# Readout scratch, two-part triangles, modulation on ScalarE and the order of fills in a two-layer diffusion block

## The chip, the cores and the metric

One Trainium2 chip; the program runs on one of its cores. The metric is device time of one execution in microseconds (us). The median of three executions of the kernel before is 2352.65 us.

## The reference

Two layers of a diffusion block over 512 latent tokens and 256 context tokens (together 768 columns), width 1024, all in fp32:

```python
def trunk_layer(x, xc, c, c_ctx, ada_w, ada_b, norm_g, w_in, ..., ctx_out):
    mod = jax.nn.silu(c) @ ada_w + ada_b
    mod_c = jax.nn.silu(c_ctx) @ ada_w + ada_b
    shift, scale, gate = jnp.split(mod[:, None, :], 3, axis=-1)
    ...
    h = rms_norm(x, norm_g) * (1.0 + scale) + shift
    za, ga, zb, gb, zc, gc, zg = jnp.split(h @ w_in, list(IN_CUTS), axis=-1)
    ya, yac = rwkv7_branch(za, zac, ...)            # recurrence, both directions
    yb = dense_block_attention(qb_, k of zbc and zb, v of zbc and zb)       # MLA
    yc = window_attention(qc_, kc_, vc_, kcc, vcc, c_sink)                  # GQA
    x_new = x + gate * merge_branches((ya, yb, yc), (ga, gb, gc), zg, w_branch_out, w_out)
    ...                                             # the same for the context, in layer 0 only

def rwkv7_scan(r, decay, k, v, kk, a, s0, reverse):
    def step(S, inp):
        r_t, w_t, k_t, v_t, kk_t, a_t = inp
        sa = jnp.einsum('bhvk,bhk->bhv', S, kk_t)
        S = (S * w_t[:, :, None, :] - sa[..., None] * (kk_t * a_t)[:, :, None, :]
             + v_t[..., None] * k_t[:, :, None, :])
        return S, jnp.einsum('bhvk,bhk->bhv', S, r_t)
    ...
```

Each branch output is multiplied by its own SiLU gate (`ga`, `gb`, `gc`), projected, weighted by sigmoid gates of `zg`, summed and projected once more.

## The kernel before

**Stages of a layer.** `head` makes the modulated input `hh`, `hl` (a high and a low part; every large product is made of three, high by high, high by low, low by high). `zphase` makes the inputs of the recurrence. `rwkv` runs the recurrence in 12 chunks of 64 steps, both directions and all heads at once. Then come MLA (`mla`), GQA (`gqa`), the projections of the branches and the last projection (`tail`).

**Fills.** The projections that nobody needs at once are a list of tiles (`todo` in `tiles`, lines 1457 to 1467): `zb` (MLA), `zc` (GQA), the gate tiles `ga`, `gb`, `gc` and 24 tiles of `zg`. A tile is 8 pieces; in the second layer a piece is 3 products of 128x512 for most tiles. `pace(n)` (line 1471) traces the next n pieces at the point where it is called, to give TensorE work while the other engines prepare something. `FILL` (line 33) says how many at which point: 72 and 56 in the second layer before the chunk loop begins, then per chunk at three stops. A raw tile is read from PSUM by ScalarE (line 778); a SiLU tile by ScalarE and then VectorE (lines 780, 782).

**Order.** A scheduler orders the instructions of each engine when the program is compiled: among those that it holds to be ready, the one with the lowest band number goes first (`band(SERVE)` before `band(B + 1)`, and so on to `B + 4` for fills); emission order decides only inside a band. The engines then work their queues in order. Two things bind the order further. `tc.issue_after(x)` ties what is traced inside behind x on x's engine. And `in_line()` (line 148) ties every product on TensorE behind the product traced just before it, whatever stage that belonged to, since `line["last"]` is set by every product and every transposition of the program:

```python
    def queued(i):
        if line["on"] and line["last"] is not None:
            tc.add_manual_dep(i.ins, line["last"].name, ...)
        line["last"] = i.ins
```

The chunk loop of `rwkv` and the last steps of the first inverse run inside `in_line()` (line 538).

**The recurrence.** For each chunk, `rwkv_scores` loads `BK`, `AR` and `UV` (lines 611 to 625) on SP's queue and makes the scores (`scps`); `rwkv_step` makes `Rp`, `Up`, `Sp` and `Yp`. Scores run two chunks ahead of the step. `AR` has 4 places, and so has `UV`. `rwkv_inverse` inverts the triangles of four chunks: it loads them as `TT` (lines 659 to 664, four loads), transposes the two diagonal 32x32 blocks on VectorE (670), eliminates in 30 steps of two VectorE instructions (676 to 681), transposes (684, 685), and then TensorE makes the block below the diagonal (`zp`, line 694, reading the other block of `TT`, and `yp`, line 702). One `TT` place, so the next group's load waits for the last `zp`. The first inverse runs in band B + 1 before the loop, the others in band B + 2.

`readout` (line 567) normalises finished columns, after chunks 3, 9 and 11 in the first layer and 9 and 11 in the second. Its scratch `tmp` (line 578) takes one `AR` place; its loads of `bvd` and the gate take `UV` places (599).

**Modulation.** `ada` (line 224) makes the modulation. With `pool` (before the first `head`) it works in 512 columns; otherwise, as `side`, in 16 halves of 256 columns that are stepped along between the pieces of other products in the first layer: 8 products `modps`, a VectorE copy to `row` (261), 4 transpositions `modpt`, and a VectorE addition of the bias into `mod` (269 or 272). `modps` and `modpt` share one PSUM place.

**GQA tokens.** `gqa_tokens` (line 1115, second layer called at line 1493 in band B + 3, before `rwkv`) takes six blocks of 128 tokens; in the second layer blocks 0 and 1 have keys and values only. Per block: loads `raw` from `zb_d` (1161, two places) on SP, transpositions `gqm` (1169), squares on ScalarE into `x` (1172), sums and rotation on VectorE (1173, 1143, 1147) and POOL (1149), a store of `x` (1177). In the second layer `x`, its helper and the PSUM place are single.

Of the kernel before, what the change touches and what calls it, by code (L numbers as in the profile page):

```python
# [10 lines left out]
F32 = mybir.dt.float32  # L11
# [3 lines left out]
ALU = mybir.AluOpType  # L15
# [4 lines left out]
P = 128  # L20
# [11 lines left out]

FILL = ((48, 48, 2, (2, 2, 2), (3, 3, 3), 2), (72, 56, 4, (2, 2, 2), (3, 3, 3), 2))

# [26 lines left out]
def build(tc, A, out):  # L61
# [162 lines left out]
    def ada(l, pp, mod, parts, pool=None):  # L224
# [25 lines left out]
        for q, h in [(q, h) for q in parts for h in range(512 // n)]:  # L250
            ps = bank([P, n], "modps")

            for k0 in range(0, KT, 4):
                with band(SERVE):
                    ws = four(q, h, k0)
                    for i in range(4):
                        mm(ps[32 * i:32 * i + 32], sc2[:, k0 + i, :], ws[i], start=(k0 == 0), stop=(k0 + 4 == KT),
                           skip_group_check=True)
                yield
            row = spool.tile([P, T], F32, tag="st", name="row", bufs=2)  # L260
            V.tensor_copy(row[:, 0:n], ps)
            nf = n // P
            pt = bank([P, nf, 2], "modpt")
            for i in range(nf):
                mm(pt[:, i, :], row[:, i * P:(i + 1) * P], C["sum4"])
            if q < 4:
                m, b = (a.rearrange("p (s f) c -> p s f c", s=2)[:, h:h + nf // 2, 2 * q:2 * q + 2]
                        for a in (mod[:, 0:16], pp[:, o:o + 16].unsqueeze(2)))
                V.tensor_tensor(m, pt.rearrange("p (s f) c -> p s f c", s=nf // 2), b.to_broadcast([P, nf // 2, 2, 2]), ALU.add)
            else:  # L270
                f = 4 * q + 2 * h
                V.tensor_tensor(mod[:, f:f + nf], pt, pp[:, o + f:o + f + nf].unsqueeze(2).to_broadcast([P, nf, 2]), ALU.add)

# [235 lines left out]

    def rwkv(l, D, last, DL, B, pace, zlast):  # L510

        with tc.tile_pool(name="rw", bufs=1, reuse_waits="tile") as rp:
# [23 lines left out]
            with band(B + 4), tc.issue_after(zlast):  # L536
                pace(FILL[l][1])
            with band(B + 1), in_line():
                for _ in ahead:
                    pace(FILL[l][2])  # L540
                ahead = out = iter(())
                for i in range(NCH):
# [9 lines left out]
                    step = rwkv_step(l, last, i, yo, st, DL, rp, parts.pop(i), YB[i // NS])  # L552
                    for n in FILL[l][3 if i % NS < NS - 1 else 4]:
                        next(step, None)
                        next(nxt, None)
                        if i % NS == NS - 1:
                            next(ahead, None)
                        next(out, None)
                        pace(n)
# [7 lines left out]
    def readout(l, D, rp, yo, part):  # L567
# [9 lines left out]

        tmp = rp.tile([P, 6, 256], F32, tag="AR", name="ro", bufs=4)
        def spread(p):
            ps = psum_bcast(256)  # L580
            mm(ps, bones, tmp[:, 4 + p % 2])
            V.tensor_scalar(tmp[:, p], ps, 1.0 / 64, None, ALU.mult)

        for p in range(4):
            y = cols(yo[:, p])
            ps = psum_bcast(256)
            mm(ps, C["center"], y)
            S.copy(y, like(ps, y))
            S.activation(like(tmp[:, 4 + p % 2], y), y, AF.Square)
            if p:  # L590
                spread(p - 1)
            yield
# [64 lines left out]
    def rwkv_inverse(l, rp, g, YB):  # L657

        TT = rp.tile([P, 8, NS, 64], F32, tag="TT", name="TT")
        cs = slice(g * NS, (g + 1) * NS)  # L660
        for b0 in (0, 64):

            DMA.dma_start(TT[b0:b0 + 32], tt_d[l][b0:b0 + 32, :, cs])
            DMA.dma_start(TT[b0 + 32:b0 + 64, :, :, 0:32], tt_d[l][b0 + 32:b0 + 64, :, cs, 32:64])
        yield
        inv = rp.tile([P, 1536], F32, tag="inv", name="inv")
        MB, tmp = inv[:, 0:1024], inv[:, 1024:1536]
        YK = YB[:, :, 32:64]
        TT4 = TT.rearrange("p c s t -> p (c s) t")
        V.transpose(MB, TT4[:, :, 0:32].rearrange("p n j -> p j n"))  # L670

# [18 lines left out]
        for n0 in range(0, 32, 16):  # L690
            zp = rps.tile([P, 16, 32], F32, tag="r", name="zp", bufs=RB)
            for n in range(16):
                for b0 in (0, 64):
                    mm(zp[b0 + 32:b0 + 64, n, :], TT4[b0:b0 + 32, n0 + n, 32:64], X13[b0:b0 + 32, n0 + n, :])
            z3 = tmp.rearrange("p (n j) -> p n j", j=32)
# [742 lines left out]
    for l in range(2):  # L1438
# [18 lines left out]
        def tiles():  # L1457
# [4 lines left out]
                          for n, t in enumerate((T_GA, T_GB, T_GC)))  # L1462
            todo = (zb[2:] + zc[4:] + zc[:4] + zb[:2] if last else zb + zc) + ga + gb
            todo += gc + [(T_ZG + j, th_zg[l][j], segs, "tanh") for j in range(24)]
# [6 lines left out]
        def pace(n):  # L1471

            for _ in zip(range(n), steps):
                pass
# [15 lines left out]
        if last:  # L1490
            cctx.close()
            with band(B + 3):
                gqa_tokens(l, F, last, ss)
        rwkv(l, D, last, DL, B, pace, zlast)
        weights["queue"] = getattr(nc, QUEUES[l][2])
        with band(B + 4), tc.issue_after(line["last"]):
            pace(22 * 8 - sum(FILL[l][0:2]) - 2 * FILL[l][2] - NG * (3 * sum(FILL[l][3]) + sum(FILL[l][4])) - 4 * FILL[l][5])

# [162 lines left out]
```

## Time and profile before

| | us |
|---|---|
| median of 3 executions | 2352.65 (2346.26 to 2353.32) |
| profiled execution, its own time | 2353.25 |
| its span, first to last instruction | 2351.5 |
| TensorE (PE) busy | 2096.9 |
| VectorE (DVE) busy | 1267.4 |
| ScalarE (ACT) busy | 890.7 |
| GpSimd (POOL) busy | 865.6 |
| mean granted clock of TensorE | 0.95 of full speed |

The recurrence of the first layer lies at about 411 to 684 us of the span, that of the second at about 1677 to 1891; the stretch of `zphase` and of fills comes before each. In a timeline row the columns are start, length, engine, line, operation, output and inputs, count, and in brackets how long the engine was idle before it and who ended that. SPq is SP's queue of DMA issues.

### The profile page before, as it was taken

Reading aid. Unit: us, or ns where it says so; the run is one execution under the profiler, and the core shown is the slowest. Engines: PE = TensorE matmul, PEld = TensorE weight load, DVE = VectorE, ACT = ScalarE, POOL = GpSimd, SP = SyncE. Lnnn points to the kernel's source line nnn. Section 1 sums busy time; section 2 is a strip of 40 time slices with the busy share of each in tenths; the row PEclk is TensorE's granted clock in tenths of the full one; section 3 lists DMA queues with packets and bytes.
Section 4 is the critical chain, followed back from the end, with each engine's and each line's share of the span. In section 5 each row is a group of like instructions: output and inputs, shape, how many; then the busy total and the mean of one; then the engine's idle time right before and its main releaser. Section 6 shows DMA issues by size and latency. Waiting matters only on the chain. (4 is left out here: it accounts for less than half of the span.)

```text
span 2351.5 us, 42314 instructions
## 1 busy us (share of the span) xinstructions
PE 2096.9 (89%) x16680; PEld 1623.2 (69%) x16680; DVE 1267.4 (54%) x2300; ACT 890.7 (38%) x1654; POOL 865.6 (37%) x699
## 2 busy tenths in 40 slices
PE   6986898888989999989699998889878998999989
PEld 3865676776877766766478876668657876666657
DVE  4476315547436666337537255742668357565643
ACT  3543212233346333354232245433333455534422
POOL 1355312111122344444362324554211145455663
PEclk9998899898999999999899999999989998999999
DMA  7146566554242111431173413566554262215344
GB/s 254 59 137 185 174 201 200 131 144 127 85 132 75 57 41 52 155 121 46 51 238 126 146 61 92 162 201 189 147 127 122 74 215 82 82 50 188 104 156 140
DMA packets 321223, 301.63 MB, mean 128 GB/s; under 512 B 111744, under 2 KB 234368, under 8 KB 321024
## 3 DMA queue, kind: packets, MB, share of 16 engines
q1 hardware_dynamic: 303216, 269.29, 38.3%
q10 hardware_dynamic: 17808, 29.63, 3.9%
q8 instruction: 132, 2.16, 0.4%
q14 instruction: 67, 0.55, 0.1%
HBM read 207.34 MB, written 91.49 MB: 127 GB/s over the span
## 5 line engine op out<-in xcount | busy, mean ns | idle before, releaser
L166 POOL TENSOR_TENSOR wl<-wf,wh 128x512 fp32r<-128x512 f32 x316 | 423.7, 1342 | 999.9 <-ACT wh L165 915.9
L154 PE MATMUL g<-hh,wh 128*128 128x512 f32 (+1 forms) x1264 | 469.2, 372 | 14.5 <-DVE st L782 6.3
L154 PE MATMUL g<-hh,wl 128*128 128x512 f32 (+1 forms) x1264 | 456.1, 361 | 4.1 <-POOL wl L166 4.0
L154 PE MATMUL g<-hl,wh 128*128 128x512 f32 (+1 forms) x1264 | 455.0, 360 | 0.0
L165 ACT CAST wh<-wf 128x512 fp32r<-128x512 f32 x316 | 195.2, 619 | 447.4 <-PE g L154 216.3
L154 PEld LDWEIGHTS g<-hh,wh 128*128 128x128 f32 x1264 | 248.9, 197 | 63.2 <-issue 10.8
L154 PEld LDWEIGHTS g<-hh,wl 128*128 128x128 f32 x1264 | 249.0, 197 | 43.6 <-issue 7.6
L154 PEld LDWEIGHTS g<-hl,wh 128*128 128x128 f32 x1264 | 249.2, 197 | 37.0 <-issue 8.8
L892 POOL TENSOR_TENSOR acc<-acc,pe 128x512 f32<-128x512 f32 (+2 forms) x128 | 145.2, 1135 | 118.0 <-ACT pe L888 98.6
L888 ACT ACTIVATE pe<-stp 128x256 f32<-128x256 f32 (+2 forms) x224 | 114.5, 522 | 190.4 <-PE stp L154 180.2
L870 DVE TENSOR_REDUCE mx<-mps 128x1 f32<-128x384 f32 (+2 forms) x256 | 124.8, 533 | 60.8 <-PE mps L154 60.1
L154 PE MATMUL g<-yh,wh 128*128 128x512 f32 (+1 forms) x224 | 79.3, 357 | 21.4 <-ACT yh L1345 17.7
L154 PE MATMUL yps<-pe,vh 128*64 128x256 f32 (+1 forms) x704 | 95.8, 381 | 1.3 <-ACT tb L900 1.2
L912 DVE RECIPROCAL rec<-sps 128x256 f32<-128x256 f32 (+1 forms) x48 | 70.3, 1478 | 35.3 <-PE sps L154 35.1
L645 DVE TENSOR_TENSOR AR<-scps,cst 64x256 f32<-64x256 f32 x96 | 40.1, 418 | 88.6 <-PE scps L154 87.4
L892 POOL TENSOR_TENSOR acc<-pe 128x512 f32<-128x512 f32 (+1 forms) x48 | 53.2, 1109 | 89.8 <-ACT pe L888 84.3
L154 PE MATMUL g<-yl,wh 128*128 128x512 f32 (+1 forms) x224 | 80.8, 361 | 5.7 <-POOL yl L1346 5.7
L154 PE MATMUL gc<-hh,wh 128*128 128x512 f32 x192 | 76.8, 400 | 8.7 <-ACT hh L325 4.6
L154 PE MATMUL g<-yh,wl 128*128 128x512 f32 (+1 forms) x224 | 79.0, 356 | 0.0
L154 PE MATMUL gc<-hl,wh 128*128 128x512 f32 x192 | 78.1, 407 | 0.1
L154 PE MATMUL scps<-AR,BK 64*128 64x128 f32 (+1 forms) x768 | 63.0, 291 | 15.8 <-DMA AR<-ard 13.5
L679 DVE TENSOR_TENSOR inv<-inv,YB 128x30 f32<-128x30 f32 (+9 forms) x180 | 70.2, 390 | 10.7 <-issue 5.1
(388 smaller groups left out, 4352.6 us busy)
## 6 DMA issues: line engine op xcount, KB each, us to landing
wf<-w_in SPq DMA_DIRECT2D x163, 256.0 KB, 2.9
wf<-ada_w SPq DMA_DIRECT2D x84, 256.0 KB, 4.2
wf<-w_in ACTq DMA_DIRECT2D x77, 256.0 KB, 3.0
bkd<-bk SPq DMA_DIRECT2D x16, 768.0 KB, 6.4
zt<-thzg SPq DMA_DIRECT2D x48, 256.0 KB, 3.1
wf<-w_bo SPq DMA_DIRECT2D x40, 256.0 KB, 2.8
thzg<-st SPq DMA_DIRECT2D x24, 384.0 KB, 2.4
vd<-t SPq DMA_DIRECT2D x64, 96.0 KB, 2.4
```

The source lines that it names most:

```text
L154: queued(TE.matmul(o, l, r, start=start, stop=stop, **kw))
L165: S.copy(wh, w32)
L166: eng.tensor_tensor(wl, w32, wh.bitcast(F32), ALU.subtract)
L645: V.tensor_tensor(AR[oth, pds, 2 * par, :], ps[oth, :, a0:a0 + 64], msk("ms", oth), ALU.mult)
L679: V.tensor_tensor(t3, M3[:, j:j + 1, 0:j].to_broadcast([P, n, j]), YK[:, j + 1:32, j:j + 1].to_broadcast([P, n, j]), ALU.mult)
L870: V.tensor_reduce(mx, ps, AX.X, ALU.max)
L888: S.activation(e, st, AF.Exp, scale=scale)
L892: G.tensor_tensor(acc, keep.pop(0, acc), e, ALU.add)
L912: V.reciprocal(rec, sps)
```

## The change

Five parts. (1) `ada` without `pool`: the copy to `row` and the addition of the bias go to ScalarE, the latter as two activations. (2) `readout`: its scratch is a tile of its own with 4 x 256 instead of 6 x 256 columns. (3) `rwkv_inverse`: `TT` is half as large and loaded twice, first the diagonal blocks in four loads, and after the transposition of these the other block in two loads. (4) `FILL` of the second layer has 3 pieces per stop in the first three chunks. (5) In the second layer the gate tiles `ga` come before `zc[:4]`, and `gqa_tokens` is traced inside `rwkv`, behind the 56 pieces and ahead of `in_line()`.

```diff
-FILL = ((48, 48, 2, (2, 2, 2), (3, 3, 3), 2), (72, 56, 4, (2, 2, 2), (3, 3, 3), 2))
+FILL = ((48, 48, 2, ((2, 2, 2),) * 3, (3, 3, 3), 2), (72, 56, 4, ((3, 3, 3), (2, 2, 2), (2, 2, 2)), (3, 3, 3), 2))
...
             row = spool.tile([P, T], F32, tag="st", name="row", bufs=2)
-            V.tensor_copy(row[:, 0:n], ps)
+            (V.tensor_copy if pool else S.copy)(row[:, 0:n], ps)
...
-            if q < 4:
+            if pool:
...
             else:
-                f = 4 * q + 2 * h
-                V.tensor_tensor(mod[:, f:f + nf], pt, pp[:, o + f:o + f + nf].unsqueeze(2).to_broadcast([P, nf, 2]), ALU.add)
+                f = 8 * h + 2 * q if q < 4 else 4 * q + 2 * h
+                for i in range(nf):
+                    S.activation(mod[:, f + i, :], pt[:, i, :], AF.Identity, bias=pp[:, o + f + i:o + f + i + 1])
...
             with band(B + 4), tc.issue_after(zlast):
                 pace(FILL[l][1])
+            beside()
             with band(B + 1), in_line():
                 for _ in ahead:
                     pace(FILL[l][2])
...
-                    for n in FILL[l][3 if i % NS < NS - 1 else 4]:
+                    for n in FILL[l][3][i // NS] if i % NS < NS - 1 else FILL[l][4]:
...
-        tmp = rp.tile([P, 6, 256], F32, tag="AR", name="ro", bufs=4)
+        tmp = rp.tile([P, 4, 256], F32, name="ro")
+
         def spread(p):
             ps = psum_bcast(256)
-            mm(ps, bones, tmp[:, 4 + p % 2])
+            mm(ps, bones, tmp[:, p])
...
-            S.activation(like(tmp[:, 4 + p % 2], y), y, AF.Square)
+            S.activation(like(tmp[:, p], y), y, AF.Square)
...
-        TT = rp.tile([P, 8, NS, 64], F32, tag="TT", name="TT")
+        TT = rp.tile([P, 8, NS, 32], F32, tag="TT", name="TT")
         cs = slice(g * NS, (g + 1) * NS)
-        for b0 in (0, 64):
-
-            DMA.dma_start(TT[b0:b0 + 32], tt_d[l][b0:b0 + 32, :, cs])
-            DMA.dma_start(TT[b0 + 32:b0 + 64, :, :, 0:32], tt_d[l][b0 + 32:b0 + 64, :, cs, 32:64])
+        for b0 in range(0, P, 32):
+
+            DMA.dma_start(TT[b0:b0 + 32], tt_d[l][b0:b0 + 32, :, cs, b0 % 64:b0 % 64 + 32])
         yield
...
+        V.transpose(MB, TT.rearrange("p c s t -> p t (c s)"))
+
+        TT = rp.tile([P, 8, NS, 32], F32, tag="TT", name="TT")
+        for b0 in (0, 64):
+            DMA.dma_start(TT[b0:b0 + 32], tt_d[l][b0:b0 + 32, :, cs, 32:64])
         TT4 = TT.rearrange("p c s t -> p (c s) t")
-        V.transpose(MB, TT4[:, :, 0:32].rearrange("p n j -> p j n"))
...
-            todo = (zb[2:] + zc[4:] + zc[:4] + zb[:2] if last else zb + zc) + ga + gb
+            todo = zb[2:] + zc[4:] + ga + zc[:4] + zb[:2] + gb if last else zb + zc + ga + gb
...
-        if last:
-            cctx.close()
-            with band(B + 3):
-                gqa_tokens(l, F, last, ss)
-        rwkv(l, D, last, DL, B, pace, zlast)
+        if last:
+            cctx.close()
+
+        def tokens():
+            if last:
+                with band(B + 3):
+                    gqa_tokens(l, F, last, ss)
+
+        rwkv(l, D, last, DL, B, pace, zlast, tokens)
```

## Rows read from the trace of the kernel before

**Rows 1.** The page, busy time of each engine, with its share and instructions.
```profile
PE 2096.9 (89%) x16680; PEld 1623.2 (69%) x16680; DVE 1267.4 (54%) x2300; ACT 890.7 (38%) x1654; POOL 865.6 (37%) x699
```

**Rows 2.** Waits of TensorE: total us, times, longest us.
```profile
PE zp L154 <- DVE inv L685: 15.1, 3, 10.8
...
PE scps L154 <- DMA AR<-ard: 13.5, 3, 7.2
...
PE modps L154 <- DVE mod L272: 6.8, 4, 6.1
...
PE g L154 <- DVE st L782: 6.3, 4, 3.1
...
PE modpt L154 <- DVE row L261: 3.8, 3, 3.0
...
PE gqm L157 <- ACT x L1176: 3.2, 1, 3.2
```

**Rows 3.** Windows: length, busy PE, PEld, DVE, ACT, POOL, PEclk, DMA share, GB/s.
```profile
478.10:482.00 3.90, 3.87 (x29) 2.84 (x31) 1.12 (x1) 0.55 (x1) 1.89 (x2) 0.50 0.40 133
...
568.70:576.20 7.50, 7.49 (x57) 5.88 (x57) 4.68 (x8) 3.20 (x4) 2.83 (x3) 0.55 0.48 132
...
1677.00:1689.00 12.00, 12.00 (x280) 10.05 (x280) 1.38 (x2) 5.06 (x9) 4.47 (x4) 0.82 0.26 78
...
1740.50:1752.00 11.50, 10.25 (x249) 8.75 (x249) 3.37 (x8) 4.43 (x8) 3.16 (x3) 0.75 0.24 73
```

**Rows 4.** Groups by form: busy us, mean ns, idle before, releaser.
```profile
L261 DVE COPY row<-modps 128x256 f32<-128x256 f32 x16 | 6.7, 419 | 20.9 <-PE modps L154 20.9
...
L272 DVE TENSOR_TENSOR mod<-modpt,pp 128x4 f32<-128x4 f32 x8 | 1.3, 158 | 15.4 <-PE modpt L154 15.4
...
L118 ACT ACTIVATE sc<-c 128x16 f32<-128x16 f32 x1 | 0.2, 218 | 0.0
...
L778 ACT COPY st<-g 128x256 f32<-128x256 f32 x14 | 5.2, 373 | 45.7 <-PE g L154 42.0 <-POOL wl L166 3.7
```

**Rows 5.** Timeline of TensorE, both layers.
```profile
554.80 1.15 PE L154 MATMUL Yp<-AR,So 64*64 64x64 f32 x32
...
1676.96 1.91 PE L154 MATMUL zp<-inv,TT 32*32 32x32 f32 x64 [6.41 <-issue]
...
1938.26 0.40 PE L157 MATMUL gqm<-cst,raw 128*128 128x128 f32 x2
```

**Rows 6.** Timeline of SP's queue of DMA issues.
```profile
555.99 0.57 SPq L618 DMA_DIRECT2D AR<-ard  x1
...
565.53 0.58 SPq L620 DMA_DIRECT2D AR<-ard  x1
...
1669.91 1.09 SPq L1161 DMA_DIRECT2D raw<-zbd  x2
...
1930.96 0.33 SPq L1177 DMA_DIRECT2D qkvd<-x  x1
```

**Rows 7.** DMA issues: count, KB each, median us from issue to landing.
```profile
raw<-zbd SPq DMA_DIRECT2D x64, 64.0 KB, 2.6
...
qkvd<-x SPq DMA_DIRECT2D x10, 384.0 KB, 3.0
...
TT<-ttd SPq DMA_DIRECT2D x12, 256.0 KB, 4.4
TT<-ttd SPq DMA_DIRECT2D x12, 128.0 KB, 4.5
```

**Rows 8.** Window of fill products `g` alone, columns as in rows 3.
```profile
1624.00:1640.00 16.00, 16.00 (x72) 13.25 (x71) 0.69 (x1) 1.17 (x2) 1.00 0.64 176
```

**Rows 9.** Timeline of ScalarE: squares of two token blocks.
```profile
1925.73 0.60 ACT L1172 ACTIVATE x<-gqm 128x512 f32<-128x512 f32 x1 [1.12 <-DMA qkvd<-x]
...
1935.28 0.59 ACT L1172 ACTIVATE x<-gqm 128x512 f32<-128x512 f32 x1
```

## The prediction before the result

> **What bounds the kernel now.** I read the page's engine list first: TensorE is busy 89% of the span and the next engine 54% [rows 1]. So work taken from another engine is worth nothing by itself; only idle time of TensorE can be won or lost, some 255 us in all, and it is worth asking which wait owns it. The second view is the list of TensorE's waits. Four of its rows belong to places that the change touches: modulation products waiting for VectorE's read of the sums before (6.8 us, 6.1 of it in one wait), modulation transposes waiting for VectorE's row copy (3.8, one of 3.0), score products waiting for the load of `AR` (13.5, one of 7.2), and the first products behind the inverse, `zp`, waiting for VectorE (10.8 in one wait) [rows 2]. The third view is windows around these waits, for one more price: behind a long wait the granted clock is low for a while. After the 6.1 us wait it is 0.50 for 3.9 us, a loss of 1.95 us; after the `AR` wait 0.55 for 7.5 us, 3.4 us; after the 10.8 us wait 0.75 for 11.5 us, 2.9 us [rows 3]. A long stall costs its length plus 2 to 3 us. Last come timelines of TensorE, of SP's queue and of ScalarE, to see in which order things stand.
>
> **Part 1, modulation read by ScalarE.** Sixteen row copies and sixteen small additions (8 parts in 2 halves) leave VectorE in the first layer. The 6.1 us wait arises because a 0.158 us addition stands behind the inverse's transposes in VectorE's queue. On ScalarE it is two instructions of at least 0.218 us (the nearest row is 128x16), and the copy costs 0.373 instead of 0.419 [rows 4]. So each chain is 2 x 0.218 - 0.158 - 0.046 = 0.23 us longer, at most 16 x 0.23 = 3.7 us on TensorE, at least nothing where a fill product stands between; I take 1.5, as fills stand between most of them. The wait shrinks from 6.1 to about 0.6 (-5.5) and its slow clock goes (-1.9); VectorE is free again when the next UV copy needs it. Of the 3.0 us wait for a row copy I take 2. Sum -5.5 - 1.9 - 2 + 1.5, about -8. Bounds -11 and +4: ScalarE's queue also holds the weight casts, which POOL and then TensorE wait for, and they now stand behind copies that wait for TensorE. Weights are four buffers ahead, so I stay near the gain.
>
> **Part 2, the readout's scratch in its own place.** Until now it takes one of the four `AR` places while chunks 4 and 5 run. SP's timeline shows the result: an `AR` load starts at 555.99, as the products that read an older `AR` (554.80 to 555.95) end, and its last part goes out only at 565.53, as loads of the readout have come between [rows 5, 6]. TensorE waits 7.2 us for it. With a place free the load can start some 20 us earlier. The readouts of chunks 9 and 11 take no place from anyone, since no chunk beyond 11 is loaded, so this is worth one stall: -7.2 and -3.4 of slow clock [rows 2, 3], of which I take -10. Next late would be the inverse of the third group, which VectorE has done well ahead there. Bounds -11 and 0 (the readout's `ro2` tiles still compete for `UV`).
>
> **Part 3, triangles in two parts.** Each of six inverses gets two more loads, and the second part waits for VectorE's transposition of the first. Behind it on SP's in-order queue stand score loads and, in the first layer, weights; the waiters are TensorE's scores and ScalarE's casts. The second part is needed only after the 30 elimination steps, so it lies beside VectorE's work; if that cover goes, its landing of about 4.5 us is paid. By the rows a load in pieces of 128 bytes (the 128 KB ones) lands in 4.5 us, one in long pieces (256 KB) in 4.4 [rows 7]: equal times for half the bytes. I take +1 in all; bounds -1 and +6.
>
> The Trainium skill, DMA: Bandwidth & Descriptors, Specifications, wants transfers of at least 512 B for full rate, and the change cuts 1 KB runs to 128 B. By that rule the first part would take about twice as long per byte, which the equal landing times above do bear out; as the bytes per load halve too, the sum would stay as it is.
>
> **Part 4, more fill in the second layer's first group.** Three steps get 3 pieces for 2 at each of 3 stops: 9 pieces of 3 products of 512 columns. 72 such products take 16.0 us [rows 8], so 27 take 6.0 us. They move from the stretch after the recurrence into the time before the 10.8 us wait, which ends when VectorE ends the second inverse and not before. -6.0, and about half of the 2.9 us of slow clock: -7.5. Bounds -9 and 0 (if the added fill delays VectorE's start).
>
> **Part 5, the order of fills and the place of the GQA tokens.** This decides the sign. SiLU-gated fills leave the stretch in which VectorE inverts, so waits of fills for `st` go (6.3 us in the whole run, most of it there [rows 2]); but they only bring TensorE sooner to the end of the 56 pieces. `gqa_tokens` now stands between these pieces and the block in which each product is tied behind the product traced before it. So the first `zp` of the block is tied behind the last transposition of token block 5. Before, `zp` ran at 1676.96 and that transposition at 1938.26 [rows 5]. Nothing else can fill TensorE meanwhile: later fills are tied behind `zp`, and their weights hold the weight buffers. How long is the chain? The first raw load goes out at 1669.91, behind the loads of chunks 2 to 4, which have the higher priority and keep it [rows 6]. It lands 2.6 us later [rows 7]; with issue and transposition ScalarE starts at about 1673.3. A full block is 9.55 us after the one before, as there is one `x` and its store must land (squares at 1925.73 and 1935.28, the store between at 1930.96 [rows 9, 6]); four blocks, so three such distances, 28.7. The first two blocks are keys and values only; no row shows them alone, so each costs between a store (0.33 and 3.0 us [rows 6, 7]) with some 0.9 of arithmetic, 4.2, and a full 9.55; I take 5, as the arithmetic is short. The last transposition starts 3.0 us behind its square and takes 0.40 [rows 5, 9]. Sum 1673.3 + 10 + 28.7 + 3.4 = 1715.4, against 1677.0: +38. The loads can come some 2 us earlier since the fills before them do: +36, and +1 for a longer slow clock than the 0.82 over 12 us behind today's `zp` [rows 3]. Bounds: 0 if the loads find room 38 us earlier, +47 with two full blocks at the start. In return the tokens leave the end of the recurrence: the wait of 3.2 us there [rows 2], 28 transpositions that no longer stand among fills (14 pairs at 0.40 us at most; I take 3), and 1 us of a lighter SP queue: -7.
>
> **Sum.** -8 - 10 + 1 - 7.5 + 36 + 1 - 7 = +5.5. The profiled execution took 2353.25 us (span 2351.5), 0.6 above the median of 2352.65. So 2358 us. Its own range, from the spread of the token chain (8 either way) and of parts 1 to 4 (9), is 2344 to 2372.
>
> **Rivals.**
> (a) The token chain is hidden: SP has room for the raw loads some 35 us earlier, while 56 pieces of fill run. For it speaks that keys and values are stored long before; against it that today's raw loads also came only at 1669.91, though nothing but the queue held them. Without the 37 us: 2358 - 37 = 2321. The chain from the first raw load to the last transposition is 45.5 us, so it decides once that load stands before about 1632.
> (b) Slower: the chain is longer. The first two blocks cost as much as full ones (+9), and the raw loads fall behind the second triangle parts, which wait for VectorE's transposition (an estimate of +3, as the queue has other work meanwhile): 2370. It decides if the last transposition comes after 1724.
> (c) The scratch doesn't do what it says: the `AR` load still goes out behind the readout's loads, as SP serves in order and `UV` is still shared. Part 2 is then 0: 2368.
> If part 1 goes wrong in ScalarE's queue, 12 us are added to any of these.
>
> **How the numbers follow.** The forecast, 0.53; (a) 0.27; (b) 0.12; (c) 0.08. A measurement of this kernel can tell 0.3%, 7 us, from no change: 2345.6 to 2359.7. The forecast straddles the upper bound: of its 0.53 some 0.24 lie above, 0.22 within, 0.07 below. Faster 0.07 + 0.27 = 0.34; same 0.22 and a little of (c), 0.23; slower 0.24 + 0.12 + 0.07 = 0.43. Cases of both signs hold much, so the range reaches into both: 2318 to 2378.
>
> **What would show it.** In the profile after: no wait of `modps` for the additions above 1 us; no wait of `scps` for `AR` near 565; the wait of `zp` of group 1 down from 10.8 to about 5; and in the second layer all ten groups of `gqm` before the first `zp`, behind an idle stretch of some 40 us at a low clock. If `gqm` runs among the 56 pieces, part 5 is wrong and (a) holds; if the time is lower although the idle stretch is there, parts 1 to 4 were sized too small.

## The result and the profile after

The changed kernel takes 2426.2 us (median of four, 2416.9 to 2432.2) against 2350.2 us before: a ratio of 1.0302, 95% interval 1.0274 to 1.033. It is 3% slower, 76 us, and 48 us above the upper end of the predicted range. The profiled execution is the fastest of the four, 2416.9 us with a span of 2415.1, so the traces account for 63.6 of the 76 us. TensorE's work is the same; its share fell [rows 1]:

```profile
PE 2108.3 (87%) x16680; PEld 1633.0 (68%) x16680; DVE 1260.9 (52%) x2268; ACT 903.8 (37%) x1702; POOL 865.8 (36%) x699
```

The waits of TensorE in the kernel after (total, times, longest), to be held against [rows 2]. The code is shifted by some lines (the inverse's last transposition L685 is now L691, `st` L782 is L788):

```profile
PE zp L154 <- DMA TT<-ttd: 21.0, 3, 11.0
...
PE gqm L157 <- issue: 17.7, 4, 4.8
...
PE gqm L157 <- DMA raw<-zbd: 13.9, 6, 10.3
...
PE zp L154 <- DVE inv L691: 11.2, 2, 5.8
...
PE gqm L157 <- ACT x L1182: 9.0, 5, 2.7
PE g L154 <- DVE st L788: 8.7, 4, 7.2
PE scps L154 <- DMA AR<-ard: 8.7, 2, 7.8
...
PE modps L154 <- ACT mod L273: 6.2, 4, 4.0
```

Two families are new. One is the `gqm` rows, 41 us together: they are the wait of the in-line block for the token blocks, called the gate below, which the prediction put at 36. The other is the first row, `zp` waiting for the load of `TT`, and the prediction has nothing like it: it gave the two-part triangles 1 us, at most 6. TensorE's timeline shows where both lie (start, length, instruction, idle time before it and its releaser):

```profile
509.96 0.28 PE L154 MATMUL zp<-inv,TT 32*32 32x32 f32 x2 [11.04 <-DMA TT<-ttd]
...
610.96 1.91 PE L154 MATMUL zp<-inv,TT 32*32 32x32 f32 x62 [9.64 <-DMA TT<-ttd]
...
1714.12 0.69 PE L157 MATMUL gqm<-cst,raw 128*128 128x128 f32 x2 [10.32 <-DMA raw<-zbd]
...
1748.74 0.66 PE L157 MATMUL gqm<-cst,raw 128*128 128x128 f32 x2 [4.52 <-issue]
1749.33 1.92 PE L154 MATMUL zp<-inv,TT 32*32 32x32 f32 x64
...
1817.51 1.92 PE L154 MATMUL zp<-inv,TT 32*32 32x32 f32 x64 [5.77 <-DVE inv L691]
```

In the second layer the last fill ends at 1703.80 and the first `zp` starts at 1749.33, right behind the last of the tied `gqm`: 45.5 us, where it was 6.4 [rows 5]. In the first layer the `zp` of groups 1 and 2 wait 11 and 9.6 us. Windows of the kernel after around the first and the last of these show the clock (columns as in [rows 3]):

```profile
498.92:509.96 11.04, 0.00 (x1) 0.03 (x1) 1.51 (x4) 0.12 (x1) 1.26 (x1) 0.65 0.99 190
...
512.43:523.85 11.42, 10.01 (x197) 8.50 (x196) 2.89 (x6) 3.88 (x8) 0.00 (x0) 0.80 0.03 5
...
1703.80:1749.33 45.53, 8.42 (x30) 4.69 (x29) 13.57 (x34) 8.22 (x18) 8.77 (x10) 0.54 0.36 98
1749.33:1761.78 12.45, 11.82 (x219) 9.60 (x218) 2.22 (x6) 8.43 (x14) 3.83 (x4) 0.77 0.31 83
```

Why the second triangle part is late stands in the queue of SP. Its rows in the kernel after, first part, second parts of groups 1 and 2, and the first raw load of the tokens:

```profile
440.54 0.56 SPq L666 DMA_DIRECT2D TT<-ttd  x1
...
505.41 1.83 SPq L675 DMA_DIRECT2D TT<-ttd  x2
...
606.72 0.63 SPq L675 DMA_DIRECT2D TT<-ttd  x1
...
1708.87 1.09 SPq L1167 DMA_DIRECT2D raw<-zbd  x2
```

and in VectorE's timeline, the transposition that frees the place:

```profile
444.18 1.96 DVE L671 STREAM_TRANSPOSE inv<-TT 128x1024 f32<-128x1024 f32 x1 [1.03 <-DMA TT<-ttd]
```

The place is free at 446.1; the load goes out at 505.4, 59 us later, and not for want of a free place. Between 441 and 505 SP issues 35 loads of scores for later chunks. These are traced in band B + 1, and so is the first part; the second part is in band B + 2 with the rest of the inverse, so the scheduler puts the scores first. SP's waits between 441 and 506 show what holds the queue up meanwhile (total, times, longest):

```profile
SPq L162 <- PE modps L154: 13.2, 3, 5.9
SPq L246 <- POOL wl L166: 9.5, 4, 3.1
SPq L790 <- DVE inv L685: 9.1, 1, 9.1
```

With smaller ones SP waits 35 us, all of it ahead of loads of weights (lines 162 and 246) and of stores (790), none ahead of the 35 score loads. The second part goes out behind all of these. In the second layer the same load of group 1 goes out 36 us after its place is free (1775.6 to 1811.7), and there `zp` still waits for VectorE and not for the load: the elimination covers it.

The account of the 63.6 us, by the same marks in both traces: the first layer and all up to the second layer's first scores +29.4 (1605.72 to 1635.08); from there to the first `zp` of the second layer +43.0 (71.24 to 114.25); from that `zp` to the one of group 1 +4.6 (63.56 to 68.18); everything behind it -13.4.

### The profile page after: what moved, and what is told of

Its sections match the earlier page's. It is cut to its first block, busy times and chain, and to the rows that moved or that the text cites. A ratio compares the mean times of both kernels' runs of the same rounds, so it can differ in the third digit from the quotient of the medians.

```text
span 2415.1 us, 42334 instructions
## 1 busy us (share of the span) xinstructions
PE 2108.3 (87%) x16680; PEld 1633.0 (68%) x16680; DVE 1260.9 (52%) x2268; ACT 903.8 (37%) x1702; POOL 865.8 (36%) x699
## 5 line engine op out<-in xcount | busy, mean ns | idle before, releaser
L786 ACT ACTIVATE st<-g 128x256 f32<-128x256 f32 (+1 forms) x108 | 56.6, 524 | 57.8 <-PE g L154 56.3
L687 DVE TENSOR_TENSOR YB<-YB,inv 128x30 f32<-128x30 f32 (+9 forms) x180 | 74.5, 414 | 5.4
```

The source lines that it names most:

```text
L687: V.tensor_tensor(YK[:, j + 1:32, 0:j], YK[:, j + 1:32, 0:j], t3, ALU.add)
L786: S.activation(t[:, sl], p, AF.Tanh, scale=0.5)
```

## The experiments

Two theories were put against their rivals first. **G**: the gate costs what the second layer shows. **Q**: the second part is late because of its place in SP's queue.

**The tie alone undone (a_no_tie).**

```diff
         def tokens():
             if last:
+                keep = line["last"]
                 with band(B + 3):
                     gqa_tokens(l, F, last, ss)
+                line["last"] = keep
```

> The changed kernel, but the memory of the last product is put back after the tokens are traced: the first zp of the in-line block is tied behind the last of the 56 fill pieces again, no longer behind the last transposition of token block 5. Theory G (the gate costs what the trace of after shows: last fill to first zp 45.5 us against 6.4 before, and the slow clock behind it): about 43 us of the changed kernel's 2426 go, less the 7 us of tokens at the end of the recurrence that I credited: 2426 - 43 + 5 = 2388, and the first zp of the second layer follows the last fill by under 10 us. Rival O (it is the new order of the fills, whose st products hold TensorE and VectorE at the start of the second recurrence, and not the tie): 2415 or more, with zp still some 30 us behind the fills. The 21 us of zp waiting for the load of TT in the first layer stay in either case.

2381.7 us, 1.0108 of before (1.008 to 1.0135). In its TensorE timeline the gate is gone, and the other family stays:

```profile
513.46 0.28 PE L154 MATMUL zp<-inv,TT 32*32 32x32 f32 x2 [11.14 <-DMA TT<-ttd]
...
1708.08 1.92 PE L154 MATMUL zp<-inv,TT 32*32 32x32 f32 x64 [1.17 <-issue]
```

From the second layer's first scores to this `zp` 69.65 us pass, against 114.25 with the tie: 44.6 us, and the ratios of the two kernels differ by 0.0194, which is 46 us. G holds; O falls.

**The second part at the priority of the score loads (b_second_band).**

```diff
-        for b0 in (0, 64):
-            DMA.dma_start(TT[b0:b0 + 32], tt_d[l][b0:b0 + 32, :, cs, 32:64])
+        with band(10 * l + 1):
+            for b0 in (0, 64):
+                DMA.dma_start(TT[b0:b0 + 32], tt_d[l][b0:b0 + 32, :, cs, 32:64])
```

> The changed kernel, but the loads of the second part of the triangles have the priority of the score loads (B + 1) and not that of the inverse (B + 2). Theory Q (in the changed kernel SP sends the second part behind all score loads of later chunks, since those have the higher priority; TensorE then waits 11.3 and 9.6 us for it in groups 1 and 2 of the first layer, and runs at a low clock behind it): these waits go, and with the clock some 13 to 16 us for each of the two: 2426 - 30 = 2396, range 2388 to 2404. Rival W (the load takes long whatever its place, or the wait only moves to the scores, because SP now waits for VectorE's transposition with the score loads behind it): 2415 to 2430, with new waits of scps for AR or of DVE for BK.

2400.0 us, 1.0191 (1.0153 to 1.023): 26 us gone, no `zp` waits for `TT` any more. Q holds. But W has a part too. SP's queue in this run:

```profile
446.13 0.57 SPq L676 DMA_DIRECT2D TT<-ttd  x1
...
450.91 0.56 SPq L676 DMA_DIRECT2D TT<-ttd  x1
...
452.96 0.63 SPq L621 DMA_DIRECT2D AR<-ard  x1
```

and TensorE behind it:

```profile
457.76 0.76 PE L154 MATMUL scps<-AR,BK 64*128 64x128 f32 x2 [10.30 <-DMA AR<-ard]
```

The `AR` loads now stand behind the two second parts, and the scores that waited 6.3 us there in the kernel before (3.2 and 3.1) and 7.8 in the kernel after wait 11.8.

**Both edits (c_both).**

> Both of the edits above in one kernel. If theories G and Q both hold and their places do not overlap (first layer, second layer), the gains add: 2426 - 38 - 30 = 2358, and against the kernel before it is what parts 1, 2 and 4 bring, less the two more loads of each triangle: 2340 to 2362. If O or W holds it stays above 2385.

2350.3 us, 0.9977 (0.9959 to 0.9996). The two faults are the whole loss: without them the change is 0.2% faster than the kernel before. What is missing is the rest of the predicted gain; parts 1, 2 and 4 were to bring 25 us.

**Part 5 alone on the kernel before (d_part5).**

> The kernel before with part 5 alone: the new order of the second layer's fills and the tokens traced just ahead of the in-line block, with the tie that this brings. Theory G: 2350 + 43 - 6 = 2387, with a wait of about 45 us between the last fill and the first zp of the second layer, and no change ahead of 1600 us. Rival: the gate shows only because the first raw loads stand behind the second part of the triangle; without that part the loads find room earlier and the time is below 2370.

2393.7 us, 1.0159 (1.013 to 1.0188). Its timeline has the first `zp` behind a gap of 40 us (the last fill ends at 1675.71):

```profile
1715.81 1.92 PE L154 MATMUL zp<-inv,TT 32*32 32x32 f32 x64
```

So the gate does not need the second triangle part. The part costs 37.6 us net. In its trace 107.7 us pass from the second layer's first scores to this `zp`: 36.5 more than before, where the full change has 43.0 more.

**Part 1 alone (e_part1).**

> The kernel before with part 1 alone (modulation read by ScalarE). Theory M (the step as I predicted it): the 6.1 us wait of modps near 478 falls to about 0.6, or to 1.2 as in the run with both edits, its slow clock goes: 8 us faster than before (5 to 11), with no other row of the first layer more than 1 us later. Rival: the additions now stand behind ScalarE's two copies of YB (2.1 us together), which wait for VectorE's transposition, as one did in the changed kernel (wait of 4.0 us): 3 us faster or less.

2352.1 us, 0.9988 (0.9967 to 1.0008): some 3 us, where 8 were expected, not told from none. The wait that was aimed at has gone, and others have come:

```profile
372.95 0.39 PE L154 MATMUL g<-hh,wh 128*128 128x256 f32 x1 [1.01 <-ACT wh L165]
...
474.61 0.64 PE L154 MATMUL modps<-wf,sc 128*32 128x256 f32 x8 [0.50 <-ACT mod L273]
...
572.25 2.05 PE L154 MATMUL scps<-AR,BK 64*128 64x128 f32 x14 [8.79 <-DMA AR<-ard]
```

6.1 us became 0.5, but the `AR` wait that part 2 was to remove grew from 7.2 to 8.8, fills wait for casts that stand behind ScalarE's new copies, and the first `zp` waits 4.5 us for VectorE instead of 2.3. In the full change the wait of `modps` was still 4.0 us: there the addition stood behind ScalarE's two copies of `YB`.

**Part 4 alone (f_part4).**

> The kernel before with part 4 alone (27 more products of fill in the second layer's first group). Theory F: they go into the 10.8 us wait of zp of group 1, whose end VectorE sets: that zp comes no later than at 1742, the wait falls to about 5, the run is 7 us faster (5 to 9). Rival: VectorE's inverse is itself pushed back by the later steps, zp of group 1 comes 4 us later or more, and the run gains 3 us or less.

2355.7 us, 0.9996 (0.9978 to 1.0015): nothing. The two `zp` in its timeline:

```profile
1683.50 1.92 PE L154 MATMUL zp<-inv,TT 32*32 32x32 f32 x64 [6.47 <-issue]
...
1750.94 1.92 PE L154 MATMUL zp<-inv,TT 32*32 32x32 f32 x64 [2.84 <-DVE inv L685]
```

67.4 us lie between them, 63.6 before. The wait fell by 8.0 us, but VectorE ended its inverse 3.9 us later. One reason shows in VectorE's timeline, two steps of nearly the same size:

```profile
1724.49 0.40 DVE L681 TENSOR_TENSOR YB<-YB,inv 128x228 f32<-128x228 f32 x1
1724.92 1.36 DVE L679 TENSOR_TENSOR inv<-inv,YB 128x234 f32<-128x234 f32 x1
```

and beside it, on POOL, the low half of a weight of the fills:

```profile
1724.58 1.44 POOL L166 TENSOR_TENSOR wl<-wf,wh 128x512 fp32r<-128x512 f32 x1 [5.64 <-ACT wh L165]
```

Among the 180 elimination steps of the second layer 10 are about 1 us too long in the kernel before and 15 in this run, and every one overlaps a `wl` of POOL. In the inverse of group 1 itself none is held before and three are in this run, 3.2 us together; VectorE's transposition starts 0.8 us later too.

**The mirror of part 4 (p_fill1):** one piece per stop for two in that group.

> The kernel before with the second layer's first group given 1 piece at each stop for 2: 9 pieces fewer, the mirror of part 4. If VectorE ends the second inverse at its own time (my step for part 4), zp of group 1 comes 63.6 us behind zp of group 0, as before, and waits 10.8 + 6.0 = 17 us. If each piece in this stretch pushes VectorE's inverse back (by part 4's run 3.9 us for 9 pieces), the distance falls to about 60 us and the wait stays near 13.

```profile
1754.54 1.92 PE L154 MATMUL zp<-inv,TT 32*32 32x32 f32 x64 [15.26 <-DVE inv L685]
```

The distance is 64.6 us, and one step is held in this inverse: with fewer fills VectorE nearly keeps its own time, as my step said; with more it does not. (The one time, 2372.8, is not used: 13 us of it lie ahead of the place of the edit, where the code is the same, and I can't say why.)

**Parts 2 and 3, with the second part early (h2_parts23_band) and as in the change (h_parts23).**

> The kernel before with parts 2 and 3 alone (scratch in a place of its own, triangles in two parts), the second part loaded at the priority of the score loads, so that it is not late. Theory S (my sum for parts 2 and 3): the wait of scps for AR near 565 goes and nothing takes its place: 9 us faster. Rival D (two more loads that wait for VectorE's transposition stand in SP's queue ahead of the AR loads of chunk 2 and 3): the wait of scps near 447 grows from 6.3 us to about 12, the first zp of the first layer comes 3 us later, and the run is within 3 us of before.

> The kernel before with parts 2 and 3 alone, just as in the change: the second part of the triangles at the priority of the inverse. Theory Q: the waits of zp for TT in groups 1 and 2 of the first layer (about 11 and 9 us) appear here too, without parts 1, 4 and 5, and the run is 26 us slower than the one with the higher priority: 2378 against 2352. Rival: without part 1 ScalarE's and SP's order is another, and the second part is not late: within 8 us of before.

Early: 2352.5 us, 0.9986 (0.997 to 1.0002). As in the change: 2381.6 us, 1.0101 (1.0076 to 1.0127), 27 us apart by the ratios, and TensorE's timeline of the latter has the waits of Q without the other parts:

```profile
500.68 0.28 PE L154 MATMUL zp<-inv,TT 32*32 32x32 f32 x2 [10.73 <-DMA TT<-ttd]
```

The early one misses S's 9 us (its interval ends at 7) and does not pay as D said. In its trace the `AR` wait of the first chunks is short and the one near 565 is another, short one:

```profile
458.17 2.04 PE L154 MATMUL scps<-AR,BK 64*128 64x128 f32 x14 [2.37 <-DMA AR<-ard]
...
568.84 1.13 PE L154 MATMUL scps<-AR,BK 64*128 64x128 f32 x14 [1.76 <-DVE TR L648]
```

With part 1 as well the `AR` wait of the first chunks was 11.8 us (b_second_band). What part 1 does to these loads was not followed.

**Parts 1 to 4 without part 5, second part early (i_1234band).**

> The kernel before with parts 1 to 4, the second part of the triangles loaded at the priority of the score loads, and without part 5. Against the run with both edits it lacks the new order of the fills and the later place of the tokens. Theory A (the parts' own gains add: -4 of part 1, -3.5 of parts 2 and 3, 0 of part 4, from their runs): 7 us faster than before, 2 us better than with both edits. Rival N (the new order of the fills brings something by itself): 4 us or more slower than the run with both edits.

2351.4 us, 0.9979 (0.9966 to 0.9991), the same as with both edits: the new order of the fills is worth nothing that these runs can tell, and the parts' small gains about add.

**The second part from POOL's queue: ahead of the select (k_1234pool), behind it (k2_pool_late).**

```diff
         G.affine_select(YK, MB.rearrange("p (j i) -> p j i", i=32), ...)
+        for b0 in (0, 64):
+            G.dma_start(TT[b0:b0 + 32], tt_d[l][b0:b0 + 32, :, cs, 32:64])
```

> The kernel before with parts 1 to 4, without part 5; the second part of the triangles is loaded from POOL's queue instead of SP's. There the instruction behind it (the select of YB) waits for the same transposition of VectorE, so the load holds nobody up. If rival D of the run before is right, this takes its price away: the wait of scps near 447 is back at 6.3 us, no zp waits for TT, and the parts give -8 - 10 - 6: about 20 us faster than before (12 to 26). If parts 1, 2 and 4 are worth nothing by themselves, within 6 us of before.

> Parts 1 to 4 with the second part loaded from POOL's queue as in the run that was 22 us slower, but issued behind the select of YB and not ahead of it. Theory H (there POOL took the two issues, 1 us each and 3 us apart, ahead of the select on which VectorE's elimination waits, so each inverse ended 6 us later or more and zp waited 11.6, 9.4 and 3.2 us in the first layer): the select is back within 3.5 us of the transposition, the waits of zp in groups 0 to 2 fall below 3 us, and the run is 8 us faster than before (4 to 14). Rival I (loads issued by POOL slow VectorE for as long as they run, wherever they stand): still 12 us slower than before or more.

Ahead: 2378.0 us, 1.0085 (1.0061 to 1.011), against 20 us of gain expected. My expectation had overlooked what stands behind the load on its engine. POOL's timeline:

```profile
382.99 1.14 POOL L674 DMA_DIRECT2D TT<-ttd  x1 [1.61 <-DVE inv L670]
386.15 1.28 POOL L166 TENSOR_TENSOR wl<-wf,wh 128x512 fp32r<-128x512 f32 x1 [2.02 <-ACT wh L165]
387.38 0.96 POOL L674 DMA_DIRECT2D TT<-ttd  x1
388.17 1.46 POOL L678 TENSOR_SCALAR_AFFINE_SELECT YB<-inv 128x1024 f32<-128x1024 f32 x1
```

The transposition ended at 382.7; the select, on which the elimination waits, came 5.5 us later, and the first `zp` waited 11.6 us. Behind the select: 2355.0 us, 0.9989 (0.9975 to 1.0002). H is right on the first layer's groups 1 and 2 (their `zp` wait 0.2 us), not on group 0 (4.6 us), and the `AR` wait there is 2.7 us, but the 8 us did not come: in the second layer fills wait for VectorE four times (6.1 us, 4.3 before), the `zp` lie 67.4 us apart, and the stretch behind the second of them takes 610 us, as before (611), where i_1234band has 599. Rival I falls.

**POOL's queue in the first layer, SP's in the second (r_mixed); low halves by VectorE in the second layer's recurrence (q_low_dve); both (s_mixed_low).** In the first of these the loads stand behind the select `if not l` and in `band(10 * l + 1)` otherwise; the second sets the engine of `wl`:

```diff
-        eng.tensor_tensor(wl, w32, wh.bitcast(F32), ALU.subtract)
+        weights.get("low", G).tensor_tensor(wl, w32, wh.bitcast(F32), ALU.subtract)
...
+            if last:
+                weights["low"] = V          # until the recurrence ends
             with band(B + 4), tc.issue_after(zlast):
```

> Parts 1 to 4; in the first layer the second part of the triangles is loaded from POOL's queue behind the select (that run's first layer, from the first zp to krp, took 285.9 us, the one with SP at the higher priority 292.8), in the second layer by SP at the higher priority. Theory Z (what the SP loads cost in the first layer is their place ahead of the AR loads of chunk 2): the wait of scps near 450 is 3 us and not 12, the first layer's stretch takes 286 us, and the run is 10 us faster than before (6 to 14). Rival: the difference of the two first layers is chance from run to run; within 6 us of before.

> Parts 1 to 4 with the second part at the higher priority (the run that was 0.21% faster than before), but in the second layer's recurrence the low halves of the weights (wl) are computed by VectorE instead of POOL. In the traces so far each elimination step of VectorE that takes about 1 us longer than its like (15 of 180 in the second layer) lies beside a wl of POOL. Theory X (the two hold each other up): with no wl on POOL there the stretched steps fall from 15 to 3 or fewer; the inverses lose some 12 us and get some 20 wl of 0.69 us back (the nearest row: st of 128x512), so the time stays within 5 us. Rival Y (the steps are stretched by something else that comes with the weights, their transfers for one): 10 or more stretched steps remain, and the run is 8 us slower or more.

> The two edits of the last runs in one kernel: in the first layer the second part of the triangles from POOL's queue behind the select, in the second layer wl by VectorE during the recurrence. They lie in different layers, so their gains should add: the run with the first was 0.5% faster than before, the second was 4 us better than the same kernel without it, though within its scatter. Expected 2341, 0.5 to 0.7% faster than before; if the 4 us were chance, 0.5% or less.

r_mixed: 2344.6 us, 0.995 (0.9931 to 0.9968); its scores near 450 wait as Z said, and POOL's select stands first:

```profile
452.02 1.13 PE L154 MATMUL scps<-AR,BK 64*128 64x128 f32 x14 [2.62 <-DMA AR<-ard]
```

```profile
383.52 1.26 POOL L680 TENSOR_SCALAR_AFFINE_SELECT YB<-inv 128x1024 f32<-128x1024 f32 x1 [1.18 <-DVE inv L670]
384.74 1.12 POOL L684 DMA_DIRECT2D TT<-ttd  x1
```

q_low_dve: 2347.2 us, 0.9974 (0.9955 to 0.9993), and not one of the 180 steps is stretched (15 in the same kernel without the edit). X holds. The row of the inverse of group 1 in VectorE's groups:

```profile
L166 DVE TENSOR_TENSOR wl<-wf,wh 128x512 fp32r<-128x512 f32 x7 | 4.8, 686 | 1.3 <-ACT wh L165 1.3
```

The gain lies ahead of the first inverse's end (first scores to first `zp` 67.1 us for 71.2); in group 1 the stretching and the added arithmetic cancel (66.3 us for 66.6 between the `zp`). Both together: 2340.2 us, 0.9929 (0.9903 to 0.9954), the best version found, 0.7% faster than the kernel before and, by the ratios, 3.6% faster than the changed one.

The first layer's recurrence from the first `zp` to `krp` (the first product of the MLA stage behind it) gives the placement of the second part in one table (the runs by the first letters of their names). Kernels whose first layer has the same code agree within 8 us, which is also how well one trace can tell a part's gain:

| second part of the triangles | kernels | first `zp` to `krp`, us |
|---|---|---|
| none (one load, as before) | before, f, p, d | 294.0, 298.2, 299.3, 291.4 |
| none, with part 1 | e | 288.2 |
| SP, priority of the inverse | after, a | 319.4, 319.6 |
| the same without part 1 | h | 311.1 |
| SP, priority of the scores | b, c, i, q | 292.2, 292.5, 292.8, 290.7 |
| the same without part 1 | h2 | 283.9 |
| POOL, ahead of the select | k | 293.3, and its first `zp` comes 8.5 us later than in k2 |
| POOL, behind the select | k2, r, s | 285.9, 279.4, 285.8 |

The late load costs 27 us with part 1 (after against b) and without it (h against h2). That POOL's queue is better than an early place on SP's shows only among the kernels with part 1; h2, which has SP's queue and no part 1, is as short as the kernels with POOL's. No run settles whether POOL's queue gains anything by itself or only avoids what part 1 does on SP's.

The clock goes the same way. Windows of that stretch, in the kernel before, then after, then r_mixed:

```profile
410.99:704.96 293.97, 260.34 (x3881) 219.35 (x3882) 151.47 (x350) 102.49 (x182) 47.02 (x37) 0.92 0.45 124
```

```profile
413.54:732.96 319.42, 267.46 (x3882) 225.29 (x3882) 150.74 (x341) 105.36 (x196) 47.49 (x37) 0.88 0.45 114
```

```profile
417.21:696.61 279.40, 255.03 (x3881) 214.89 (x3882) 150.53 (x341) 105.30 (x196) 51.08 (x41) 0.96 0.51 129
```

The same products (3881 or 3882 of them in the trace) take 267 us of TensorE after, 260 before and 255 in r_mixed, at a mean granted clock of 0.88, 0.92 and 0.96.

## Why the prediction was wrong, step by step

**Part 3 is the step that failed.** It listed what would queue behind the second load, and priced the load's own landing at 4.5 us if its cover went. It took for granted that the load goes out when its place is free. It did not ask what the load queues behind. The code gives that away: `invert` behind its first loads runs in band B + 2, score loads in B + 1, and the lower band goes first. The price is not a landing but the whole backlog of SP, 59 us in group 1 and 57 in group 2 from a free place to the (last) issue; the elimination covers all but 11.0 and 9.6 us of it and the landing. With the slow clock behind them (0.80 for 11.4 us behind the first) that is 26 us by b_second_band and 27 by the pair of h runs, against bounds of -1 and +6. Against the forecast for the first layer (-8 - 10 + 1 = -17) the traces show +29.4: 46 of the 58 us by which the two traces miss the sum. Of these some 26 are the late load and some 12 what parts 1 and 2 did not bring (6 for 18, in their own runs); the other 8 are within what single traces can tell. The landing itself is no part of the miss: the `TT` loads landed in 4.1 us (median) in the kernel after. That 128 and 256 KB landed in equal times before does not show twice the time per byte, as the prediction read it; by the same rows loads of 64 KB and stores of 384 KB landed in 2.6 and 3.0 us [rows 7], so it can as well be a time that hardly depends on the size.

**Part 5 was right in mechanism and sign; its gate was sized right alone, and 6 us small in the full change.** All ten `gqm` groups run ahead of the first `zp`, with the blocks 8 us apart (I took 9.55), but the first raw load goes out at 1708.87, 5.1 us after the last fill ends, where it went out 0.6 us ahead of that end before and I had it 2 us earlier still. In SP's queue it stands behind the store of that last fill (1706.02) and four more loads. The stretch grew by 43.0 us where 37 were summed. In d_part5 it grew by 36.5, and there the first raw load still goes out 2.0 us ahead of the end of the last fill (1673.67 against 1675.71). Which of the other parts sets the raw loads back is not shown; the priority of the second triangle part is not it, as b_second_band has the late raw loads too (43.1 us). As a whole the part costs 37.6 us (d_part5); I had 37 - 7 = 30, and what is missing is the 7. The step on the fills failed: their waits for `st` were to go, and are 8.7 us in all for 6.3, 7.2 of it in one wait ahead of the last three pieces. Rival (a), a hidden chain, is out; the length lies between the forecast and rival (b).

**The return at the end** came out in its sum, -13.4 us behind the `zp` of group 1 against 6 of moved fill and 7 of tokens, but its two terms are not shown: the same stretch is 2.1 us shorter with part 5 alone (d_part5), 6.9 with part 4 alone (f_part4), and 12.0 with parts 1 to 4 and without part 5 (i_1234band). The agreement is luck.

**Part 4's step was wrong by its cover.** The wait "ends when VectorE ends the second inverse and not before" holds, but VectorE ends later when the fills come (+3.9 us), so of 7.5 us less than 1 was measured (the interval reaches 5). The prediction had "if the added fill delays VectorE's start" as its bound of 0; only 0.8 us arise there, and 3.1 in the elimination itself. There POOL's `wl`, which comes with each weight of the fills, holds three steps for 3.2 us together.

**Parts 1 and 2 were mis-sized.** The waits named are gone or shorter (6.1 to 0.5 us in e_part1, but 4.0 in the kernel after, where the sign that I gave was 1; near 565 no wait for `AR` is left in the kernel after), but of 8 us 3 were measured and of 9 another 3, neither told from zero with certainty; a wait that is removed brought TensorE sooner to the next one. The signs that I gave beforehand were a poor test of size: each looked only at its own wait. Rival (c) falls: the scratch does what it says. Part 2 was not run without part 3, so what it is worth alone is not shown.

The other 10 us of the miss are mostly the profiled execution, which is 9.3 us faster than the median of the kernel after. By the ratios the parts alone add to 57 us (part 1 -3, parts 2 and 3 +24, part 4 -1, part 5 +37) and the change costs 71: of the 14 between them 6.5 are the later raw loads, and the rest is not told from scatter. (The forecast's own range of 14 either way is neither the sum of the 8 and 9 that it names, 17, nor the root of the sum of their squares, 12; the time lies far outside by any of them.)

## What to carry to other kernels

Of a transfer that is split or moved, ask what it queues behind, not only what queues behind it: a load with a lower priority than later loads on an in-order queue is as late as that queue's backlog. An earlier place on the same queue took away the 26 us here. Where a load must wait for an engine, a queue whose next instruction waits for the same event is another place for it, if the load stands behind that instruction: ahead of it the kernel was 0.85% slower than before, behind it as fast as before, and 0.5% faster with that in the first layer alone. And before filling the wait for another engine with more work, count what the filling asks of that engine.

## What the runs showed of the hardware

A VectorE step with two inputs from SBUF that begins during POOL's `wl` is held until it ends, for about 1 us: 0.40 us became 1.36, in 15 of 180 steps, and in none once `wl` had left POOL. In f_part4 all 15 begin 0.02 to 0.40 us after a `wl` has begun and end 0.04 to 0.26 us after it has ended; 12 other steps overlap a `wl` but begin ahead of it, and none of them is held. The Trainium skill, SBUF — State Buffer, section "Who interferes with whom", states this: an instruction of VectorE with two SBUF inputs contends with one of GpSimd that reads SBUF, and the later one is blocked. The traces agree; I had not counted it when I added fills. VectorE takes 0.69 us for a `wl` that takes POOL 1.34 (means), so the 41 that VectorE took over in q_low_dve cost it 28 us, and the holds they replace were about 15: leaving them on POOL saved VectorE less than it seemed.

POOL needs 0.95 to 1.16 us of its own time to issue one of these loads, where SP's issue rows show some 0.6.
